# Sample step of the attention moved behind the prompt, its output projection by halves of tokens, and a scaling estimate kept in PSUM

## The chip, the cores and the metric

The kernel runs on one core of a Trainium2 chip. The metric is the device time of one execution in microseconds (us); the number compared is the median over runs. One execution is also recorded by the hardware profiler, and all rows quoted in this document come from such records. Engines are called PE (matrix products; PEld is its loading of weights), DVE (VectorE), ACT (ScalarE), POOL (GpSimd) and SP (SyncE, which issues the DMAs here). SBUF is the on-chip memory of the operands, and PSUM the accumulator memory of eight banks that PE writes and that DVE and ACT read and write.

## The reference

One inference step of a two-layer encoder on 512 prompt tokens and 64 sample tokens (576 in all), width 1024, float32. Layer 0 mixes tokens with a convolution module, layer 1 with stick-breaking attention on shared keys and values; both end in a SwiGLU feed-forward part.

```python
D_MODEL = 1024; SEQ = 512; DEC_SEQ = 64; PAST_LEN = 512
N_HEADS = 16; HEAD_DIM = 64; N_KV_HEADS = 4; GROUP = 4; D_FF = 2816; EPS = 1e-6

def rmsnorm(x, g):
    y = x * lax.rsqrt(jnp.mean(x * x, axis=-1, keepdims=True) + EPS)
    return y * g

def swiglu(xn, w_gu, w_down):
    g, u = jnp.split(xn @ w_gu, 2, axis=-1)
    return (jax.nn.silu(g) * u) @ w_down

def stick_breaking_block(q, k, v, q_pos, k_pos):
    z = jnp.einsum('bgrqd,bgsd->bgrqs', q, k) * (HEAD_DIM ** -0.5)
    mask = k_pos[None, :] < q_pos[:, None]
    log_beta = jax.nn.log_sigmoid(z)
    log_keep = jnp.where(mask, log_beta - z, 0.0)
    after = lax.cumsum(log_keep, axis=4, reverse=True) - log_keep
    att = jnp.where(mask, jnp.exp(log_beta + after), 0.0)
    return jnp.einsum('bgrqs,bgsd->bgrqd', att, v)

# in trunk(), layer 1, once for the prompt and once for the sample tokens:
    h = h + sb_attention(rmsnorm(h, b_norm_g), k_all, v_all, q_pos, k_pos, w_q, w_o)   # o @ w_o at its end
    h = h + swiglu(rmsnorm(h, ffn_norm_g[1]), w_gu, w_down)
    return rmsnorm(h, final_norm_g), ...
```

## The kernel before

Activations lie transposed: a chunk of 128 features on the partitions, the 576 tokens along the row (512 of the prompt, then 64 of the sample). A row is worked on in two halves of 288 tokens, so the second half holds the last 224 prompt tokens and all sample tokens. Each product in float32 precision is made of three in a faster format: every operand is split into a high part (ACT copies it, rounding) and a low part (DVE or POOL subtracts). A weight tile of 512 columns is split in the same way (L518 high part; L528 low part, on DVE). In the feed-forward stages a second copy of the high part is first put into a free PSUM bank (`hp`, L523), so that L528 reads one operand from PSUM; the banks for this are the list `hbanks`, in turn. The feed-forward products use sums of blocks (Strassen's way, seven products in place of eight), which POOL and DVE make (`S`, `ta`, `tb`).

The order of work on each engine is written out ahead: every step is entered as an operation with a cost, the tags that it reads and writes, and a rank; a planner (`Plan`) lays the operations of one stage on the engines by list scheduling, and the engines then run that order. An engine that waits holds up all that stands behind it. An operation that reads two SBUF operands on DVE, or runs on POOL, is entered with `port=True`: the planner doesn't let two such overlap. Stages are planned one after the other: convolution and first feed-forward; keys, values and attention; second output projection and feed-forward.

**Attention.** Ten units run one after another, each in five block steps with the stages z (scores), s (soft-plus), t (running sums), e (weights) and v (times values). A prompt unit `p` does two heads (one group of 128 features, index j = 0 to 7) for 512 tokens; a sample unit `s` does eight heads for the 64 sample tokens, that is, the last 64 columns of four indices j. `S_AT = (4, 7)` puts the sample units behind p3 and ahead of p7, so the order is p0 p1 p2 p3 s0 p4 p5 p6 s1 p7. At its end a unit adds two halves of `av` into the one buffer `oc` (ACT L2276, DVE L2279) and splits `oc` into the operand of the output projection (DVE L2294 `ob`/`oh`, POOL L2297 `ob`/`ol`): one such pair of 512 columns for a prompt unit, four of 64 columns for a sample unit. An output-projection tile `oproj(i, m)` (`pw`) is made of indices 4i to 4i+3 and adds into chunk m of the residual `h` (L759). The eight tiles with i = 0 are spread over the steps of the last two units; those with i = 1 are the mixer of the next stage.

**Entry of the second feed-forward stage.** `ffn(1, ...)` starts from an estimate of the RMS scale: squares of four chunks are summed (`ss0`), a product with ones adds over features (`cs`, banks b6 and b7), ACT turns it into `r0` (Ln L1490, Exp L1494) in an SBUF buffer, and DVE scales each finished chunk with it (`xs`, L1532: chunk, gain column, `r0`). From `xs` come the operands of the gate and up products (L1343 high parts, L1347 low parts). The right scale follows in `rest()`: the sums of all eight chunks go into b6 and b7 (L1505), DVE reads them (`ry`, L1515), multiplies by `r0` twice (L1518), and ACT and DVE make `r`, which is applied after the products. Behind `rest()`, b6 and b7 become the `hp` banks. The first gate and up tile (`pg`) takes the operands in the order of the chunks 0, 4, 1, 5, 2, 6, 3, 7; (1, c) in a tile name is the pair of chunks c and c+4 of stage 1. The next products are `j_A`, `j_B`, `j_C`.

Of the kernel before, what the change touches and what calls it, by code (L numbers as in the profile page):

```python
# [4 lines left out]
F32R = mybir.dt.float32r  # L5
# [65 lines left out]
N_HL = {"s": 4, "e": 3}  # L71
N_T = 6
T_WR = "wr2"
S_AT = (4, 7)
Y_POOL = (2, 4)
LT, LV = 1, 2
Q_AT = 2
# [144 lines left out]
def build(tc, xT, vec, st, stp, bdp, wt, ck, cv, w_in, w_out, gu, down, wk, wv, wq, wo, yT, csp, css, kp, ks, vp, vs):  # L222
# [147 lines left out]
    def pe(n):  # L370
        return n * 0.000442 + 0.004
# [118 lines left out]
    def split_unit(u, tag):  # L490
        kind, i, a, n = units[u]
        th, tl = tag.replace("w", "wh"), tag.replace("w", "wl")
        unit_at[u] = tag
        if kind == "sum":
            sums_of(i, a)
            st = X[("St", i, a)]
            le = LO_S

            def get():
                return X[("S", i, a)][:, :n]  # L500
        else:
# [12 lines left out]

        def hi():
            if not bank:
                place()
            nc.scalar.activation(X[("w", u)][0][:, :n], get(), AF.Copy)  # L518

        def hi_bank():  # L520
            place()
            t = tile(("hp", u), bank, (P, 512), F32R, pool=pp)
            nc.scalar.activation(t[:, :n], get(), AF.Copy)  # L523

        def lo():
            a, b = X[("hp", u) if bank else ("w", u)], X[("w", u)][1]
            a = a if bank else a[0]
            eng(le).tensor_tensor(b[:, :n], get(), a.bitcast(F32)[:, :n], op=ALU.subtract)  # L528
# [35 lines left out]
    def by_part(tag):  # L564
        return [(tag, 0), (tag, 1)]
# [56 lines left out]
    class Norm:  # L622
# [27 lines left out]
        def rstd(self, pair, hf=None, urgent=False, bank=None):  # L650

            key = ("cs", self.name, hf)
            halves = (0, 1) if hf is None else (hf,)
            tag = tuple(pair[q] for q in halves)

            def f():
                X[key] = {q: tile(key + (q,), pair[q], (P, 512), pool=pp) for q in halves}
# [809 lines left out]
    def ffn(l, mixer, g_next, nrm_next, x_busy, k_busy):  # L1467
# [8 lines left out]
        spots["k"] = [t for t in KT if t not in k_busy]  # L1476
        nrm = Norm(f"f{l}")
        cs = ("cs", "f", l)
        r0t = single()
        xt, xops = {}, []  # L1480

        def scale():

            newps(cs, ("b6", "b7"))
            sums_op(cs, ("b6", "b7"), [(lambda: nrm.ss(0), "ss0")])

            def f():
                r0 = spot_tile(("r0", l), r0t)
                for p, (a, n) in zip(full(X[cs]), HALVES):
                    nc.scalar.activation(r0[:, a : a + n], p, AF.Ln, bias=eps, scale=2.0 / D)  # L1490

            def g():
                r0 = X[("r0", l)]
                nc.scalar.activation(r0, r0, AF.Exp, scale=-0.5)  # L1494

            op("ACT", act(T) + 0.19, f, reads=["b6", "b7", "tbl"], writes=by_part(r0t))
            op("ACT", act(T), g, reads=["tbl"], writes=by_part(r0t))

        def rest():

            for i in (0, 1) if l else (1,):

                def f(i=i):
                    for o, (a, n) in zip(full(X[cs]), HALVES):
                        nc.tensor.matmul(o, ones, nrm.ss(i)[:, a : a + n], start=i == 0, stop=True, skip_group_check=True)  # L1505

                op("PE", 8 * pe(HA), f, reads=[f"ss{i}"], writes=["b6", "b7"], bias=99.0)

            def y():
                return X[("ry", l)][:, :T]  # L1510

            def f():
                t = tile(("ry", l), "sq1", (P, 5 * P), pool=base)
                for p, (a, n) in zip(full(X[cs]), HALVES):
                    nc.vector.tensor_scalar(t[:, a : a + n], p, 1.0 / D, EPS, op0=ALU.mult, op1=ALU.add)  # L1515

            def g():
                nc.vector.tensor_tensor(y(), y(), X[("r0", l)], op=ALU.mult)  # L1518

            op("DVE", dve(T) + 0.07, f, reads=["b6", "b7"], writes=["sq1"])  # L1520
            op("DVE", dve(T), g, reads=by_part(r0t), writes=["sq1"], port=True)
            op("DVE", dve(T), g, reads=by_part(r0t), writes=["sq1"], port=True)
            op("ACT", act(T), lambda: nc.scalar.activation(r, y(), AF.Ln), reads=["sq1", "tbl"], writes=both("r"))
            op("ACT", act(T), lambda: nc.scalar.activation(r, r, AF.Exp, scale=-0.5), reads=["tbl"], writes=both("r"))
            newton_step(r, y, T, "sq1", both("r"))
            give(r0t)

        def scaled(m):
            xt[m] = single()

            def f():
                nc.vector.scalar_tensor_tensor(spot_tile(("xs", l, m), xt[m]), h[m], col(V_FG + l * NC + m), X[("r0", l)], op0=ALU.mult, op1=ALU.mult)  # L1532

            op("DVE", dve(T, True), f, reads=H(m) + by_part(r0t), writes=by_part(xt[m]), port=True)

        def x_operands(c):
            res = []
# [21 lines left out]
            for c in (0, 1) if i == 3 and not l else (i // 2,) if i % 2 and (l or i > 3) else ():  # L1559
                x_operands(c)  # L1560
        rest()
        hbanks.extend(("b6", "b7"))
        table("silu_and_others")
        spots["x"] += x_busy
        spots["k"] += k_busy
# [160 lines left out]
    def tail(l, ops_, nrm, finished):  # L1726
# [15 lines left out]
        wi = {q: take() for q in (m, m2)}  # L1742
        for q in (m, m2):
            newps(("pd", q), tag[q])
        op("ACT", 0.0, lambda: nrm.ss(1), writes=both("ss1"))
        op("ACT", 0.0, lambda: tile(("sqc",), "sq1", (P, 5 * P), pool=base), writes=["sq1"])
        for hf, (a, n_) in enumerate(HALVES):
            sl = slice(a, a + n_)
            for q in (m, m2):
# [15 lines left out]
            nrm.rstd(("b6", "b7"), hf, True, ("b5", "b2")[hf])  # L1765
            for q in range(NC // 2):
                yk, yt = ("yo", q, hf), single("xf")

# [570 lines left out]

    todo = []  # L2340

    def oproj(i, m, tag):
        wi = take()
        k = ("pw", i, m)
        newps(k, tag)

        def deps(xk):
            j = xk[1]
            own = by_part(f"k{j - 4}") if 3 < j < 6 else by_part(f"xh{j}") + by_part(f"xl{j}") if j > 5 else []
            return [("ok", j, 0), ("ok", j, SEQ)] + oplace(j) + own  # L2350

        mm_ops(k, tag, wi, [("o", j) for j in range(4 * i, 4 * i + 4)], xdeps=deps)
        add_h(m, k, tag)

    pairs = [("p", t, 4 * t + c) for t in range(2) for c in range(4)]
# [39 lines left out]
    pp = psum_pool("pp3")  # L2395


    ffn(1, lambda i, m: oproj(1, m, (("b0", "b1"), ("b2", "b3"), ("b4", "b5"))[i % 3]), None, Norm("fin"), XT[12:], KT)
    psum.pop().close()
    ctx.close()  # L2400

# [92 lines left out]
```

## Time and profile before

| | |
|---|---|
| median of 3 runs | 1219.28 us (1218.8 to 1220.41) |
| profiled execution, its own time | 1219.93 us |
| its span, first to last instruction | 1218.2 us |
| mean granted PE clock | 0.995 |
| busy: PE, DVE, ACT, POOL | 1190.0, 1016.9, 998.1, 808.6 us |

In the rows of a timeline the columns are start, duration, engine, line, operation, output and inputs, sizes, how many instructions were merged into the row, and in brackets how long the engine sat idle ahead of it and what ended that. In the rows of windows each engine has its busy time and the number of its instructions. In the rows of groups the number behind the bar is the busy time in us, then the mean of one in ns. In the rows of waits the numbers are the total in us, how often, and the longest.

### The profile page before, as it was taken

How to read it: one execution, taken by the hardware profiler on the slowest of the kernel's cores; microseconds unless marked ns; L12 is line 12 of the kernel's file. 1: busy time of each engine (PE TensorE's matmuls, PEld its weight loads, DVE VectorE, ACT ScalarE, POOL GpSimd, SP SyncE). 2: the span in 40 equal slices, each digit the busy share in tenths (PEclk: the TensorE clock that was granted, in tenths of full speed). 3: DMA queues.
4: the chain of work that ended last, by engine and by line, in shares of the span. 5: the costliest groups of instructions: out<-in, count | busy, mean ns of one | idle time of the engine just before them, and what ended most of it. 6: DMA issues, size and time to landing. Idle time of an engine off the chain costs nothing.

```text
span 1218.2 us, 23815 instructions
## 1 busy us (share of the span) xinstructions
PE 1190.0 (98%) x8670; PEld 1161.4 (95%) x8670; DVE 1016.9 (83%) x1643; ACT 998.1 (82%) x1887; POOL 808.6 (66%) x644
## 2 busy tenths in 40 slices
PE   9999989999999999999999999998999999999996
PEld 8999989999999999999999888998999999999996
DVE  6999987979996765998679999979799966668995
ACT  7988474799888887988659999955998889889983
POOL 1999823597867876996204554454699677789951
PEclk9999999999999999999999999999999999999998
DMA  7333822123133323323364322132232424224212
GB/s 270 90 94 93 263 67 86 52 92 117 53 122 105 104 70 94 115 70 106 118 160 105 74 62 74 53 104 59 81 121 71 121 71 122 87 70 123 86 70 78
DMA packets 44997, 121.07 MB, mean 99 GB/s; under 512 B 8784, under 2 KB 14224, under 8 KB 44880
## 3 DMA queue, kind: packets, MB, share of 16 engines
q1 hardware_dynamic: 44880, 119.56, 32.4%
q8 instruction: 68, 1.11, 0.4%
q14 instruction: 49, 0.40, 0.1%
HBM read 105.18 MB, written 5.70 MB: 91 GB/s over the span
## 4 chain that ended last, share of the span: by engine, by line
PE 71%; DVE 11%; POOL 3%; issue 2%; ACT 2%; DMA 1%; SPq 0%; DVEq 0%; POOLq 0%; ACTq 0%
PE j_A L1432 29%; PE j_B L1432 15%; PE j_C L1432 7%; PE po L604 4%; PE b L2226 3%; PE pw L604 3%; PE pq L604 3%; DVE wl L528 2%; DVE acc L1065 2%; PE b L2133 1%; PE av L2253 1%; PE pk L604 1%; DMA qd<-qd 1%; PE pd L604 1%; PE pg L604 1%
## 5 line engine op out<-in xcount | busy, mean ns | idle before, releaser
L518 ACT ACTIVATE wh<-wr 128x512 fp32r<-128x512 f32 (+1 forms) x295 | 178.9, 613 | 34.3 <-PE po L604 15.2
L528 DVE TENSOR_TENSOR wl<-S,hp 128x512 fp32r<-128x512 f32 (+1 forms) x258 | 169.4, 662 | 37.7 <-ACT hp L523 35.0
L528 DVE TENSOR_TENSOR wl<-wr,hp 128x512 fp32r<-128x512 f32 (+1 forms) x233 | 154.2, 666 | 43.2 <-ACT hp L523 39.4
L518 ACT ACTIVATE wh<-S 128x512 fp32r<-128x512 f32 (+1 forms) x260 | 155.7, 610 | 8.1 <-PE j_C L1432 2.9
L523 ACT ACTIVATE hp<-S 128x512 fp32r<-128x512 f32 (+1 forms) x258 | 148.6, 580 | 11.0 <-DVE wl L528 6.3
L523 ACT ACTIVATE hp<-wr 128x512 fp32r<-128x512 f32 (+1 forms) x233 | 134.3, 579 | 16.1 <-DVE wl L528 12.4
L448 POOL TENSOR_TENSOR S<-wr,wr 128x512 f32<-128x512 f32 (+1 forms) x65 | 87.7, 1349 | 86.1 <-ACT wh L518 32.1
L1082 POOL TENSOR_TENSOR pacc<-pacc,pr 128x608 f32<-128x608 f32 x69 | 109.0, 1592 | 7.3 <-ACT pr L1079 4.1
L484 POOL TENSOR_TENSOR S<-wr,S 128x512 f32<-128x512 f32 (+1 forms) x65 | 92.1, 1418 | 26.7 <-DVE wl L528 13.4
L448 POOL TENSOR_TENSOR S<-wr 128x512 f32<-128x512 f32 (+1 forms) x65 | 88.4, 1360 | 21.6 <-ACT wh L518 9.0
L448 POOL TENSOR_TENSOR S<-S,wr 128x512 f32<-128x512 f32 (+1 forms) x65 | 91.3, 1406 | 7.3 <-DVE wl L528 6.5
L1609 POOL TENSOR_TENSOR t<-t,r 128x576 f32<-128x576 f32 x44 | 69.0, 1572 | 3.5 <-ACT t L1580 2.3
L1609 POOL TENSOR_TENSOR a<-a,r 128x576 f32<-128x576 f32 x44 | 70.2, 1599 | 1.1 <-DVE a L1586 1.1
L1065 DVE SCALAR_TENSOR_TENSOR acc<-u,vecs,acc 128x608 f32<-128x608 f32 x76 | 64.6, 850 | 1.0
L1079 ACT ACTIVATE pr<-u,vecs 128x608 f32<-128x608 f32 x69 | 54.0, 795 | 8.3 <-POOL pacc L1082 8.0
L1615 DVE TENSOR_TENSOR a<-a,t 128x576 f32<-128x576 f32 x44 | 52.3, 1188 | 8.1 <-ACT t L1613 7.7
L1580 ACT ACTIVATE t<-j_A 128x288 f32<-128x288 f32 x84 | 34.1, 406 | 23.8 <-PE j_A L1432 22.7
L528 DVE TENSOR_TENSOR wl<-wr,wh 128x512 fp32r<-128x512 f32 x62 | 48.8, 797 | 4.1 <-ACT wh L518 4.0
L2226 PE MATMUL b<-s,sums 128*128 128x512 f32 (+1 forms) x196 | 48.4, 357 | 0.0
L1665 DVE TENSOR_TENSOR h<-j_A,h 128x288 f32<-128x288 f32 x92 | 41.2, 450 | 7.0 <-PE j_A L1432 6.6
L1989 POOL COPY qs<-q 128x64 f32<-128x64 f32 x8 | 3.3, 409 | 56.3 <-DVE q L1986 56.3
L1432 PE MATMUL j_A<-('x', 0, 0)_0_b,wh 128*128 128x288 f32 x168 | 35.7, 295 | 0.5 <-ACT wh L518 0.5
(987 smaller groups left out, 4541.0 us busy)
## 6 DMA issues: line engine op xcount, KB each, us to landing
wr<-gu SPq DMA_DIRECT2D x88, 512.0 KB, 3.6
wr<-down SPq DMA_DIRECT2D x32, 512.0 KB, 3.8
wr<-w_in SPq DMA_DIRECT2D x15, 512.0 KB, 3.9
wm<-wt SPq DMA_DIRECT2D x12, 576.0 KB, 6.3
wr<-down SPq DMA_DIRECT2D x16, 384.0 KB, 3.2
qd<-qd SPq DMA_DIRECT2D x21, 256.0 KB, 2.9
wr<-w_out SPq DMA_DIRECT2D x8, 512.0 KB, 3.8
wr<-wq SPq DMA_DIRECT2D x8, 512.0 KB, 3.6
```

Of the source, the lines that this page charges most:

```text
L448: eng(e).tensor_tensor(t[:, :n], x[1](), y[1](), op=ALU.subtract if sub else ALU.add)
L484: eng(e).tensor_tensor(v[:, :n], X[("raw", i0)][:, n : 2 * n], v[:, :n], op=ALU.subtract)
L518: nc.scalar.activation(X[("w", u)][0][:, :n], get(), AF.Copy)
L523: nc.scalar.activation(t[:, :n], get(), AF.Copy)
L528: eng(le).tensor_tensor(b[:, :n], get(), a.bitcast(F32)[:, :n], op=ALU.subtract)
L604: nc.tensor.matmul(o[hf], (hi, hi, lo)[j][:, s], (xh, xl, xh)[j], start=(start and q == 0 and j == 0), stop=(stop and q == n - 1 and j == ...
L1065: nc.vector.scalar_tensor_tensor(dst, src, wt_, dst if i else X[("kneg",)], op0=ALU.mult, op1=ALU.add)
L1079: nc.scalar.activation(tile(("pr", c, i), f"pr{m}", (P, YW)), src, AF.Copy, scale=wt)
L1082: nc.gpsimd.tensor_tensor(X[("pacc", c)], X[("pacc", c)], X[("pr", c, i)], op=ALU.add)
L1432: nc.tensor.matmul(out, a[:, s], b, start=(start and q == 0 and i == 0), stop=(q == len(ops_) - 1 and i == 2), skip_group_check=True,)
L1609: nc.gpsimd.tensor_tensor(X[k], X[k], r, op=ALU.mult)
L2226: nc.tensor.matmul(out(zz()), X[(w,)], get(x), start=False, stop=(i == len(mms) - 1), skip_group_check=True)
```

## The change

The second sample unit goes to the end: with `S_AT = (4, 8)` the order is p0 p1 p2 p3 s0 p4 p5 p6 p7 s1. Each tile of the second output projection is entered as two groups of 12 matmuls, first half of tokens and then second half; the first half depends on the prompt units alone, and only the second also on the sample unit. In stage 1, `r0` is made and kept in the PSUM tile `c6` (two banks, in the place of b6 and b7), Ln and Exp writing in place; the sums of `rest()` go to b2 and b3 instead; ACT in place of DVE reads them into `ry`; `xs` and the two multiplications of `ry` read `r0` from PSUM and are entered without `port`. When the last reader of `r0` is done, `c6` is taken over as the two `hp` banks. The last norm uses the two halves of `c6` where it used b6 and b7.

```diff
-S_AT = (4, 7)
+S_AT = (4, 8)
...
         def hi_bank():
             place()
-            t = tile(("hp", u), bank, (P, 512), F32R, pool=pp)
+            if isinstance(bank, tuple):
+                X[("hp", u)] = t = X[(bank[0], "hp")][:, bank[1], :]
+            else:
+                t = tile(("hp", u), bank, (P, 512), F32R, pool=pp)
             nc.scalar.activation(t[:, :n], get(), AF.Copy)
...
-        r0t = single()
+        r0t = None if l else single()
+        r0d = both("c6") if l else by_part(r0t)
...
-            newps(cs, ("b6", "b7"))
-            sums_op(cs, ("b6", "b7"), [(lambda: nrm.ss(0), "ss0")])
+            tag = "c6" if l else ("b6", "b7")
+            newps(cs, tag)
+            sums_op(cs, tag, [(lambda: nrm.ss(0), "ss0")])
 
             def f():
+                if l:
+                    X[("r0", l)] = r0 = X[cs][:, O0 : O0 + T]
+                    nc.scalar.activation(r0, r0, AF.Ln, bias=eps, scale=2.0 / D)
+                    return
...
         def rest():
 
+            ck, ct = (("cs2", l), ("b2", "b3")) if l else (cs, ("b6", "b7"))
+            if l:
+                newps(ck, ct)
...
-                for p, (a, n) in zip(full(X[cs]), HALVES):
-                    nc.vector.tensor_scalar(t[:, a : a + n], p, 1.0 / D, EPS, op0=ALU.mult, op1=ALU.add)
+                for p, (a, n) in zip(full(X[ck]), HALVES):
+                    if l:
+                        nc.scalar.activation(t[:, a : a + n], p, AF.Identity, bias=eps, scale=1.0 / D)
+                    else:
+                        nc.vector.tensor_scalar(t[:, a : a + n], p, 1.0 / D, EPS, op0=ALU.mult, op1=ALU.add)
...
-            op("DVE", dve(T), g, reads=by_part(r0t), writes=["sq1"], port=True)
-            op("DVE", dve(T), g, reads=by_part(r0t), writes=["sq1"], port=True)
+            for _ in range(2):
+                op("DVE", dve(T), g, reads=r0d, writes=["sq1"], port=not l)
...
-            op("DVE", dve(T, True), f, reads=H(m) + by_part(r0t), writes=by_part(xt[m]), port=True)
+            op("DVE", dve(T, True), f, reads=H(m) + r0d, writes=by_part(xt[m]), port=not l)
...
         rest()
-        hbanks.extend(("b6", "b7"))
+        if l:
+            op("ACT", 0.0, lambda: tile(("c6", "hp"), "c6", (P, 2, 512), F32R, pool=pp), writes=both("c6"))
+        hbanks.extend(by_part("c6") if l else ("b6", "b7"))
...
-    def oproj(i, m, tag):
+    def oproj(i, m, tag, apart=False):
...
-            return [("ok", j, 0), ("ok", j, SEQ)] + oplace(j) + own
-
-        mm_ops(k, tag, wi, [("o", j) for j in range(4 * i, 4 * i + 4)], xdeps=deps)
+            return [("ok", j, 0)] + [("ok", j, SEQ)] * late + oplace(j) + own
+
+        xs = [("o", j) for j in range(4 * i, 4 * i + 4)]
+        if apart:
+            for hf in range(2):
+                mm_ops(k, tag, wi, xs, halves=(hf,), xdeps=lambda xk, hf=hf: deps(xk, bool(hf)), keep=not hf)
+        else:
+            mm_ops(k, tag, wi, xs, xdeps=deps)
         add_h(m, k, tag)
...
-    ffn(1, lambda i, m: oproj(1, m, (("b0", "b1"), ("b2", "b3"), ("b4", "b5"))[i % 3]), None, Norm("fin"), XT[12:], KT)
+    ffn(1, lambda i, m: oproj(1, m, (("b0", "b1"), ("b2", "b3"), ("b4", "b5"))[i % 3], True), None, Norm("fin"), XT[12:], KT)
```

More of the change, by code (lines that the diff above doesn't have):

```diff
@@ L656, in f @@
             def f():
-                X[key] = {q: tile(key + (q,), pair[q], (P, 512), pool=pp) for q in halves}
+                X[key] = {q: X[pair[q][:1]][:, pair[q][1], :] if isinstance(pair[q], tuple) else tile(key + (q,), pair[q], (P, 512), pool=pp) for q in halves}
             op("PE", 0.0, f, writes=list(tag))
@@ L1494, in g @@
                 nc.scalar.activation(r0, r0, AF.Exp, scale=-0.5)
-            op("ACT", act(T) + 0.19, f, reads=["b6", "b7", "tbl"], writes=by_part(r0t))
-            op("ACT", act(T), g, reads=["tbl"], writes=by_part(r0t))
+            op("ACT", act(T) + 0.19 * (not l), f, reads=tags(tag) + ["tbl"], writes=r0d)
+            op("ACT", act(T), g, reads=["tbl"], writes=r0d)
         def rest():
+            ck, ct = (("cs2", l), ("b2", "b3")) if l else (cs, ("b6", "b7"))
+            if l:
+                newps(ck, ct)
             for i in (0, 1) if l else (1,):
                 def f(i=i):
-                    for o, (a, n) in zip(full(X[cs]), HALVES):
+                    for o, (a, n) in zip(full(X[ck]), HALVES):
                         nc.tensor.matmul(o, ones, nrm.ss(i)[:, a : a + n], start=i == 0, stop=True, skip_group_check=True)
-                op("PE", 8 * pe(HA), f, reads=[f"ss{i}"], writes=["b6", "b7"], bias=99.0)
+                op("PE", 8 * pe(HA), f, reads=[f"ss{i}"], writes=list(ct), bias=99.0)
             def y():
@@ L1513, in f @@
                 t = tile(("ry", l), "sq1", (P, 5 * P), pool=base)
-                for p, (a, n) in zip(full(X[cs]), HALVES):
-                    nc.vector.tensor_scalar(t[:, a : a + n], p, 1.0 / D, EPS, op0=ALU.mult, op1=ALU.add)
+                for p, (a, n) in zip(full(X[ck]), HALVES):
[3 more added lines that the diff above has]
+                        nc.vector.tensor_scalar(t[:, a : a + n], p, 1.0 / D, EPS, op0=ALU.mult, op1=ALU.add)
             def g():
                 nc.vector.tensor_tensor(y(), y(), X[("r0", l)], op=ALU.mult)
-            op("DVE", dve(T) + 0.07, f, reads=["b6", "b7"], writes=["sq1"])
-            op("DVE", dve(T), g, reads=by_part(r0t), writes=["sq1"], port=True)
-            op("DVE", dve(T), g, reads=by_part(r0t), writes=["sq1"], port=True)
+            if l:
+                op("ACT", act(T) + 0.19, f, reads=list(ct), writes=["sq1"])
+            else:
+                op("DVE", dve(T) + 0.07, f, reads=list(ct), writes=["sq1"])
+            for _ in range(2):
+                op("DVE", dve(T), g, reads=r0d, writes=["sq1"], port=not l)
             op("ACT", act(T), lambda: nc.scalar.activation(r, y(), AF.Ln), reads=["sq1", "tbl"], writes=both("r"))
@@ L1525, in rest @@
             newton_step(r, y, T, "sq1", both("r"))
-            give(r0t)
+            if not l:
+                give(r0t)
         def scaled(m):
@@ L1561, in ffn @@
         rest()
-        hbanks.extend(("b6", "b7"))
+        if l:
+            op("ACT", 0.0, lambda: tile(("c6", "hp"), "c6", (P, 2, 512), F32R, pool=pp), writes=both("c6"))
+        hbanks.extend(by_part("c6") if l else ("b6", "b7"))
         table("silu_and_others")
@@ L1744, in tail @@
             newps(("pd", q), tag[q])
+        op("PE", 0.0, lambda: tile(("c6",), "c6", (P, 2, 512), pool=pp), writes=both("c6"))
         op("ACT", 0.0, lambda: nrm.ss(1), writes=both("ss1"))
@@ L1764, in tail @@
                     op("DVE", dve(n_), s, reads=["sq1", ("sq1", hf)], writes=[("ss0", hf)], port=True)
-            nrm.rstd(("b6", "b7"), hf, True, ("b5", "b2")[hf])
+            nrm.rstd(by_part("c6"), hf, True, ("b5", "b2")[hf])
             for q in range(NC // 2):
@@ L2345, in oproj, with deps @@
         newps(k, tag)
-        def deps(xk):
+        def deps(xk, late=True):
             j = xk[1]
             own = by_part(f"k{j - 4}") if 3 < j < 6 else by_part(f"xh{j}") + by_part(f"xl{j}") if j > 5 else []
-            return [("ok", j, 0), ("ok", j, SEQ)] + oplace(j) + own
-        mm_ops(k, tag, wi, [("o", j) for j in range(4 * i, 4 * i + 4)], xdeps=deps)
+            return [("ok", j, 0)] + [("ok", j, SEQ)] * late + oplace(j) + own
[3 more added lines that the diff above has]
+                mm_ops(k, tag, wi, xs, halves=(hf,), xdeps=lambda xk, hf=hf: deps(xk, bool(hf)), keep=not hf)
+        else:
+            mm_ops(k, tag, wi, xs, xdeps=deps)
         add_h(m, k, tag)
```

## The prediction

> **What bounds the kernel now.** I read the page's first part, then the windows by stage, then what PE waited for.
>
> ```profile
> PE 1190.0 (98%) x8670; PEld 1161.4 (95%) x8670; DVE 1016.9 (83%) x1643; ACT 998.1 (82%) x1887; POOL 808.6 (66%) x644
> ...
> 640.00:800.00 160.00, 159.14 (x1019) 142.35 (x1018) 153.16 (x241) 146.32 (x276) 82.27 (x71) 1.00 0.29 73
> 800.00:828.00 28.00, 26.81 (x194) 26.01 (x192) 22.17 (x36) 16.12 (x29) 14.22 (x11) 1.00 0.31 95
> 828.00:850.00 22.00, 18.55 (x125) 16.75 (x125) 22.00 (x39) 12.23 (x24) 9.41 (x6) 1.00 0.21 61
> 850.00:1190.00 340.00, 339.37 (x2558) 338.90 (x2559) 276.04 (x451) 303.63 (x609) 268.72 (x202) 1.00 0.29 93
> ```
>
> The columns of a window are PE, PEld, DVE, ACT, POOL, then PE clock, DMA share and GB/s. PE is busy for 98% of the span, and the change neither adds nor removes a matmul, so it can gain only what PE idles where it works: 0.86 us in the attention stretch (160.00 less 159.14), 1.19 us at its end (28.00 less 26.81), 3.45 us where the feed-forward stage starts (22.00 less 18.55), 0.63 us in the rest of that stage. That is 6.1 us at the very best. In the third of these windows DVE is busy for 22.00 of 22.00. The waits of PE in the two short windows:
>
> ```profile
> PE pg L604 <- DVE ('x', 1, 2)_0_b L1347: 1.7, 1, 1.7
> ...
> PE pw L604 <- POOL ol L2297: 1.2, 1, 1.2
> ...
> PE pg L604 <- DVE ('x', 1, 1)_0_b L1347: 1.1, 1, 1.1
> ...
> PE cs_f L1505 <- DVE ss_f L645: 0.5, 1, 0.5
> ```
>
> So each part of the change has a wait of its own to remove: the new order and the halves the 1.2 us on POOL's `ol`, the estimate in PSUM the 1.1 and 1.7 us on DVE's operands.
>
> **The end of the attention.** The chain behind the last step now, and the cover that PE has for it:
>
> ```profile
> 797.95 0.77 PE L2253 MATMUL av<-e,vv 128*128 128x512 f32 x2
> ...
> 800.46 0.69 PE L604 MATMUL pw<-ob,wh 128*128 128x288 f32 x4
> ...
> 801.25 0.70 PE L604 MATMUL pw<-ob,wh 128*128 128x288 f32 x4
> ...
> 805.49 0.54 PE L604 MATMUL pw<-ol,wh 128*128 128x288 f32 x2 [1.19 <-POOL ol L2297]
> ...
> 790.92 0.77 ACT L2276 ACTIVATE oc<-av 64x256 f32<-64x256 f32 x2
> ...
> 800.58 1.20 ACT L2276 ACTIVATE oc<-av 64x512 f32<-64x512 f32 x2 [2.06 <-POOL ol L2297]
> ...
> 791.79 0.85 DVE L2279 TENSOR_TENSOR oc<-av,oc 64x256 f32<-64x256 f32 x2
> ...
> 793.61 0.29 DVE L2294 CAST ob<-oc 128x64 fp32r<-128x64 f32 x2
> ...
> 795.12 1.24 POOL L2297 TENSOR_TENSOR ob<-oc,ob 128x64 fp32r<-128x64 f32 x2
> ...
> 798.12 0.32 POOL L2297 TENSOR_TENSOR ol<-oc,oh 128x64 fp32r<-128x64 f32 x1
> 798.40 1.41 POOL L645 TENSOR_TENSOR ss_f<-ss_f,sqn_f 128x576 f32<-128x576 f32 x1
> 799.78 0.77 POOL L2297 TENSOR_TENSOR ol<-oc,oh 128x64 fp32r<-128x64 f32 x1
> ...
> 803.80 1.64 POOL L2297 TENSOR_TENSOR ol<-oc,oh 128x512 fp32r<-128x512 f32 x1 [1.86 <-DVE oh L2294]
> ```
>
> p7 ends with `av` at 798.72 (797.95 plus 0.77); its `ol` is ready at 805.44, 6.7 us later, of which ACT loses 2.06 because POOL still reads `oc` for the sample unit that ran just ahead. With s1 last, nothing older sits in `oc`, and the chain is that of the sample unit: ACT 0.77, DVE 0.85, the first cast 0.15 (half of 0.29), four subtractions on POOL 1.24 + 0.32 + 0.77 = 2.33, and for five handovers some 0.1 each (805.44 to 805.49 is the shortest shown): 4.6 us. What covers it: six matmuls take 0.79 us (800.46 to 801.25), so the first halves of three tiles, 36 matmuls, take 4.7 us, and they need nothing of s1. The wait of 1.19 us is then gone. Bounds: if the written order puts only two first halves ahead (3.2 us), 1.4 us of wait stay and 0.2 is lost; if POOL's two sums of squares get between the subtractions as one does now (1.41 each), the chain is 7.4 us, the wait 2.7, and 1.5 us are lost. Above, no more than 1.19 plus a little of the 0.86 is there. I take a gain of **1.0 us**, because both terms nearly balance and the planner sees the same lengths.
>
> The unit itself is moved whole: its z, s, t, e, v steps, its split of q on POOL and its two DMAs that spread q behind it on SP come one unit later, the projection of the last queries stays with p6, and p7 takes its q from there directly, as p5 and p6 do. Such a chain costs PE little now:
>
> ```profile
> PE b L2133 <- DMA qd<-qd: 0.7, 2, 0.4
> ```
>
> I cost it at nothing; the eight tiles of `oproj(0, m)`, spread over the same steps, hide it, and without them one more wait of that sort is 0.4 us. Splitting a tile in halves adds no weight load: PEld has as many instructions as PE already (8670 each).
>
> **The entry of the feed-forward stage.** DVE works without a gap here, and what it spends:
>
> ```profile
> L1532 DVE SCALAR_TENSOR_TENSOR xs<-h,vecs,r 128x576 f32<-128x576 f32 x8 | 8.3, 1050 | 0.0
> L528 DVE TENSOR_TENSOR wl<-wr,wh 128x512 fp32r<-128x512 f32 x7 | 5.9, 854 | 0.0
> ...
> L528 DVE TENSOR_TENSOR wl<-wr,hp 128x512 fp32r<-128x512 f32 x4 | 2.7, 678 | 0.0
> L1518 DVE TENSOR_TENSOR ry<-ry,r 128x576 f32<-128x576 f32 x2 | 2.3, 1145 | 0.0
> ...
> L1515 DVE TENSOR_SCALAR ry<-cs_f 128x288 f32<-128x288 f32 x2 | 0.8, 438 | 0.0
> ...
> L1532 DVE SCALAR_TENSOR_TENSOR xs<-h,vecs,r x8: 800/966/1358, 815.8 to 839.7; 128x576 f32<-128x576 f32 x8
> ```
>
> These are groups of DVE between 810 and 860 us, and the instructions of `xs` (shortest, middle and longest in ns). The same subtraction takes 678 ns with one operand in PSUM and 854 with both in SBUF, and `xs` takes 800 ns alone and up to 1358: two SBUF operands make DVE and POOL hinder each other. With `r0` in PSUM I put `xs` at its 800: 8.3 less 6.4 is 1.9 us. The two reads into `ry` go to ACT, 0.8 us. Together 2.7 us of DVE, all of it ahead of the last of PE's waits, which sum to 2.8. Whether a PSUM operand costs DVE more is shown by
>
> ```profile
> L1780 DVE SCALAR_TENSOR_TENSOR yo<-h,vecs,rb_b x12: 503/505/508, 1206.0 to 1214.1; 128x288 f32<-128x288 f32 x12
> ```
>
> which is the same form with its last operand in PSUM: 505 ns for 288 columns. 288 more cost DVE some 0.31 us (438 ns for 288 in L1515, 0.75 us for 576 in the row of 840.96 below), which makes 815 beside the 800 from SBUF: no more than 0.1 us over all eight. [...]
>
> Against this stands a wait that the change adds. `c6` becomes the `hp` banks only when `ry` has been multiplied twice:
>
> ```profile
> 833.23 0.80 DVE L1515 TENSOR_SCALAR ry<-cs_f 128x288 f32<-128x288 f32 x2
> ...
> 840.96 0.75 DVE L1347 TENSOR_TENSOR ('x', 1, 2)_0_b<-xs,('x', 1, 2)_0_b 128x576 fp32r<-128x576 f32 x1
> ...
> 841.66 0.58 ACT L523 ACTIVATE hp<-S 128x512 fp32r<-128x512 f32 x1
> ...
> 849.85 0.40 PE L1432 MATMUL j_B<-('x', 1, 0)_0_b,wl 128*128 128x288 f32 x1
> ...
> 851.36 0.75 DVE L1518 TENSOR_TENSOR ry<-ry,r 128x576 f32<-128x576 f32 x1
> ...
> 855.36 1.54 DVE L1518 TENSOR_TENSOR ry<-ry,r 128x576 f32<-128x576 f32 x1
> ```
>
> b6 and b7 are free at 834.03 now, the first `hp` copy runs at 841.66, the multiplications at 851.36 and 855.36. They must move to some 842 us or before. Without POOL's hindrance they are 2 x 0.75 = 1.5 us. Ahead of the operand of 840.96 they eat 1.5 of the 2.7 and leave 1.2; behind it they leave 2.7. The `hp` weights feed `j_B` at 849.85 and the operand feeds `pg` at 841.76, so the planner should put the operand first. But PE then comes 3 to 4 us early to weights that ACT and DVE make without a gap:
>
> ```profile
> 845.00:850.00 5.00, 4.89 (x36) 4.51 (x35) 5.00 (x9) 5.00 (x11) 2.34 (x2) 1.00 0.21 52
> ```
>
> That is late next, and gives a part back. Between 1.2 and 2.7 I take **1.9 us**. ACT's two new reads (0.44 each, from the 438 ns of the DVE form) lie in a window where ACT is busy 12.23 of 22.00; were it full, they would cost 0.9. The first of the two sums in `rest()` now waits for L759 to free b2 and b3, ahead of `pg` on PE; the PE wait on `ss_f` (0.5 us) stands at the same place and I leave it as it is. Ln of `r0` as one instruction instead of two is worth 0.2 us on a chain of ACT that I don't count. In the last norm, b6 and b7 or the halves of `c6` are the same two banks to every instruction: nothing.
>
> **The sum.** 1.0 + 1.9 = 2.9 us of PE's idle time. The profiled execution took 1219.93 us, 1.73 more than its span of 1218.2; its span becomes 1215.3, its time 1217.0. It lay 0.65 above the median of the runs, so the median becomes 1219.28 - 2.9 = **1216.4 us**.
>
> **The rivals.** *One half only* (chance 0.33). PE's time saved at one place comes back as a wait at the other, because DVE's chain doesn't follow the earlier PE, or the written order doesn't use the first halves as cover, which is the change not doing what it says. For it: DVE has no gap between 828 and 850, and PE idled 1.19 us at 805 though tiles further on were there. Against: the 2.06 us of ACT behind `oc` vanish by the order of the units alone. With the first term only, 1218.3; with the second only, 1217.4; I give it 1218.0.
>
> *The estimate holds the banks* (chance 0.15), the slower side. If the multiplications stay where they are, the second ends at 856.90; copy 0.58, subtraction 0.68 and handovers of 0.2 bring the first weights at 858.4, 8.5 us after 849.85. Less the 2.9 gained, that is 5.6 us more, 1224.9. It decides from the point where the second multiplication ends after 845.5 (849.85 less 2.9 and 1.5): each us beyond costs one, and beyond 850.8 the kernel is slower by over 0.2%. For it: a DVE that is full. Against: the planner knows the dependence, and `ry` can be ready by 834.
>
> **How the numbers follow.** About 0.2% (2.4 us) is what a measurement of this kernel can tell from no change, so faster means below 1216.8 and slower above 1221.7. Forecast 0.52: its own range, 1.2 to 2.7 plus 1.0 to 1.2 with what is left of 0.86 and 0.63, is 1214.4 to 1217.4; 0.42 of it lies below 1216.8. The first rival gives 0.03 to faster and 0.29 to same with 0.01 slower, the forecast's upper part 0.10 to same, the second rival 0.14 to slower and 0.01 to same. Sum: 0.45 faster, 0.40 same, 0.15 slower. For 8 in 10 the range runs from 1214.4 to 1222.0, into the cheaper part of the second rival.
>
> **What would show it.** Right: PE's wait on `ol` is under 0.3 us, with 36 matmuls of `pw` between the last `av` and the first second-half matmul; `xs` stays near 800 ns in all eight; the waits on `('x', 1, 1)_0_b` and `('x', 1, 2)_0_b` sum to under 1.5 us; the second multiplication of `ry` ends before 845; the 340 us behind 850 keep an idle time near 0.6. Wrong: a new wait on the sample unit's POOL subtractions, PE waiting for `wh` or `wl` for more than 2 us after the first `pg`, or any change of more than 0.5 us ahead of 640 us, where no instruction is touched.

## The result, and the profile after

The changed kernel takes **1230.42 us** (median of 5 runs, 1227.6 to 1231.47), the kernel before, on the same chip, 1218.8 us: a ratio of 1.0095, with an interval of 1.0085 to 1.0106. It is 11.6 us slower, where 2.9 us faster was forecast, and lies outside the range. The profiled execution took 1231.47 us with a span of 1229.8.

The page's first part and the windows of the changed kernel, in the stretches that the prediction used:

```profile
PE 1194.2 (97%) x8670; PEld 1160.3 (94%) x8670; DVE 1010.5 (82%) x1641; ACT 1004.4 (82%) x1888; POOL 800.1 (65%) x644
...
640.00:800.00 160.00, 158.77 (x1014) 141.20 (x1012) 150.46 (x240) 145.39 (x275) 80.55 (x68) 1.00 0.31 75
800.00:828.00 28.00, 27.84 (x200) 27.04 (x201) 24.23 (x47) 17.16 (x30) 12.46 (x14) 1.00 0.33 103
828.00:850.00 22.00, 20.51 (x150) 19.84 (x149) 20.23 (x35) 15.48 (x32) 11.96 (x7) 1.00 0.25 73
850.00:1190.00 340.00, 329.86 (x2445) 324.62 (x2443) 263.12 (x425) 294.65 (x579) 257.24 (x197) 1.00 0.29 91
```

PE's idle time in these four stretches was 0.86, 1.19, 3.45 and 0.63 us; it is now 1.23, 0.16, 1.49 and 10.14. So the two places at which the change aims gained 1.03 and 1.96 us, and the stage behind them lost 9.51 in this window alone. Busy time doesn't tell all of it. The window holds 2445 matmuls in place of 2558, and each counts for a little more busy time (329.86 us by 2445 is 0.135, 339.37 by 2558 is 0.133). At 0.133 us each the 113 that are missing come to some 15 us, an estimate. Within that stage the loss lies in two groups of windows, with little lost between them (0.18 us of idle time from 950 to 1090):

```profile
890.00:910.00 20.00, 19.41 (x147) 19.20 (x146) 17.65 (x24) 16.43 (x33) 18.33 (x13) 1.00 0.19 54
910.00:930.00 20.00, 17.52 (x130) 17.06 (x129) 18.19 (x28) 17.93 (x36) 17.32 (x12) 1.00 0.29 90
...
990.00:1010.00 20.00, 20.00 (x153) 20.00 (x152) 13.10 (x21) 17.93 (x35) 16.48 (x13) 1.00 0.30 102
...
1090.00:1110.00 20.00, 18.41 (x133) 17.52 (x132) 13.46 (x18) 16.02 (x32) 20.00 (x17) 1.00 0.29 83
...
1150.00:1170.00 20.00, 18.58 (x138) 18.14 (x138) 18.86 (x32) 16.41 (x32) 16.77 (x15) 1.00 0.35 106
```

The kernel before has 20.00 of PE in each of these windows but the last (19.46). What PE waits for between 870 and 1190 us in the changed kernel:

```profile
PE j_A L1435 <- DVE a L1607: 4.5, 4, 2.0
PE j_A L1435 <- DVE h L1686: 2.3, 3, 0.9
PE j_B L1435 <- DVE ('a', 1, 2)_3_b L1350: 0.9, 1, 0.9
PE j_A L1435 <- ACT wh L518: 0.7, 2, 0.4
```

These are ordinary partners, late: DVE reads the products out of PSUM late (`a`, `h`), and operands and weights come late. DVE and ACT are what fell behind, though DVE was busy for less time than before (1010.5 against 1016.9 us) and ACT for only 6.3 us more (1004.4 against 998.1). What they wait for is in the view of the tile `c_hp`, the banked copies of the second gate-up stage (840 to 1210 us), here the wait of DVE for the copies and of ACT for DVE's subtraction:

```profile
  ACT c_hp L526: 67.4, 110
  DVE wl L531: 36.1, 83
```

and the same two waits in the kernel before, where the tiles are called `hp`:

```profile
  ACT hp L523: 36.2, 53
  DVE wl L528: 10.0, 20
```

The two engines wait for each other for 103.5 us instead of 46.2, and each of them is left short where it has most to do (DVE 18.19 and ACT 17.93 of 20.00 in the window at 910, with PE idle for 2.48).

**The theory from this.** Before, each banked copy is a tile of one bank, in two banks by turns. Afterwards both banks are halves of one tile, `c6`, and the waits that are put into the program take the tile as a whole: ACT's copy into one half waits until DVE has subtracted from the other, and a subtraction waits for a copy into the other half. Counted from the records, 103 of the 226 copies ran at the same time as a subtraction before, for 33.5 us together; after, none does. In the program's semaphores, 162 of the 226 copies wait for work on the other half (115 for DVE's subtraction, 47 for ACT's own copy), and 47 of the subtractions wait for a copy into the other half; in the kernel before, no copy and no subtraction waits for the other bank. **Rivals:** the estimate in PSUM itself costs (its banks, or its reads); the new order or the halves of tokens bring work to a place where it hinders; or the earlier start of the stage does.

### The profile page after: what moved, and what is told of

Same layout as the page of the kernel before. It is cut to its first block, busy times and chain, and to the rows that moved or that the text cites. A ratio compares the mean times of both kernels' runs of the same rounds, so it can differ in the third digit from the quotient of the medians.

```text
span 1229.8 us, 23801 instructions
## 1 busy us (share of the span) xinstructions
PE 1194.2 (97%) x8670; PEld 1160.3 (94%) x8670; DVE 1010.5 (82%) x1641; ACT 1004.4 (82%) x1888; POOL 800.1 (65%) x644
## 5 line engine op out<-in xcount | busy, mean ns | idle before, releaser
L518 ACT ACTIVATE wh<-wr 128x512 fp32r<-128x512 f32 (+1 forms) x295 | 178.5, 612 | 30.3 <-PE po L607 15.2
L531 DVE TENSOR_TENSOR wl<-S,c_hp 128x512 fp32r<-128x512 f32 (+1 forms) x127 | 83.8, 666 | 30.7 <-ACT c_hp L526 28.4
L531 DVE TENSOR_TENSOR wl<-wr,hp 128x512 fp32r<-128x512 f32 (+1 forms) x134 | 88.9, 667 | 20.9 <-ACT hp L526 19.8
L531 DVE TENSOR_TENSOR wl<-S,hp 128x512 fp32r<-128x512 f32 (+1 forms) x131 | 86.1, 664 | 22.4 <-ACT hp L526 21.6
L531 DVE TENSOR_TENSOR wl<-wr,c_hp 128x512 fp32r<-128x512 f32 (+1 forms) x99 | 65.6, 668 | 39.1 <-ACT c_hp L526 38.9
L526 ACT ACTIVATE c_hp<-S 128x512 fp32r<-128x512 f32 (+1 forms) x127 | 74.2, 584 | 21.0 <-DVE wl L531 18.6
L526 ACT ACTIVATE hp<-wr 128x512 fp32r<-128x512 f32 (+1 forms) x134 | 77.3, 580 | 12.3 <-DVE wl L531 9.4
L526 ACT ACTIVATE hp<-S 128x512 fp32r<-128x512 f32 (+1 forms) x131 | 75.5, 581 | 6.5 <-DVE wl L531 3.4
L526 ACT ACTIVATE c_hp<-wr 128x512 fp32r<-128x512 f32 (+1 forms) x99 | 57.8, 584 | 17.9 <-DVE wl L531 17.5
L1636 DVE TENSOR_TENSOR a<-a,t 128x576 f32<-128x576 f32 x44 | 51.5, 1171 | 12.8 <-ACT t L1634 12.4
```

Of the source, the lines that this page charges most:

```text
L1636: op("DVE", dve(T), lambda: nc.vector.tensor_tensor(X[ku], X[ku], X[kg], op=ALU.mult), reads=by_part(tg), writes=by_part(tu), port=True)
```

## The experiments

**Own tiles, and the shared tile alone.** The first experiment keeps the changed kernel and the order of instructions on every engine, and gives each banked copy a tile of one bank, out of a pool (`pph`) that takes over the place of the estimate's pool (`ppc`). The sums of the last norm, at the end of the kernel, get tiles of their own with it. The second is its mirror image: the kernel before, its order on every engine, with the second stage's copies in the halves of one tile.

```diff
# e1_apart, against the changed kernel
+    def swap():
+        own["ps"].close()
+        own["ps"] = ExitStack()
+        own["hp"] = own["ps"].enter_context(tc.tile_pool(name="pph", bufs=1, space=bass.MemoryType.PSUM, reuse_waits="tile"))
+
-    op("ACT", 0.0, lambda: tile(("c6", "hp"), "c6", (P, 2, 512), F32R, pool=pp), writes=both("c6"))
+    op("ACT", 0.0, swap, writes=both("c6"))
...
-    X[("hp", u)] = t = X[(bank[0], "hp")][:, bank[1], :]
+    t = tile(("hp", u), f"b{6 + bank[1]}", (P, 512), F32R, pool=own["hp"])
# e2_shared, against the kernel before
-    t = tile(("hp", u), bank, (P, 512), F32R, pool=pp)
+    if "hp" not in own:
+        swap()
+        own["hp"] = tile(("c6", "hp"), "c6", (P, 2, 512), F32R, pool=own["b6"])
+    X[("hp", u)] = t = own["hp"][:, int(bank == "b7"), :]
```

> The changed kernel, order of every engine untouched, but each banked copy (hp) is a tile of one bank again; c6 is given back as a whole when its last reader is done, and two separate banks take its place. Theory (one tile): the copies of ACT wait for DVE's subtraction of the OTHER half because both halves are one tile; that alone costs the 16.7 us that the changed kernel loses after its first job. Then the lead of 5.2 us at the first job stays: 1213.6, at most 1216. ACT's wait for wl falls from 36 us to under 20. Rival (order): the loss comes of the new order and of the late release of c6; the time stays at 1228 to 1231.

Measured: 1213.01 us (1212.31 to 1214.41), ratio to before 0.9959 (0.9947 to 0.9972). The same change that cost 11.6 us gains some 5 once the copies have tiles of their own. ACT's wait for the subtractions of this stage falls from 36.1 to 12.4 us.

> The kernel before, order of every engine untouched, but from the second feed-forward stage on the banked copies are the two halves of one tile. Theory (one tile): 12 to 17 us slower than before, 1231 to 1236, ACT waiting some 36 us for wl where it waited 19. Rival (order): 1218.8 as before.

Measured: 1238.68 us (1237.92 to 1244.42), ratio 1.0179 (1.016 to 1.0197). The sign is the theory's, but the time lies above what was expected, so it holds something else. What PE waits for in this run around the last projections:

```profile
PE pw L619 <- DVE oc L2303: 4.7, 1, 4.7
```

No such wait stands in the kernel before. The added pool took banks 6 and 7, so the pool of the stage's other tiles slid down to banks 0 to 5, and its first projection tile came to lie where the attention's sums `av` had been: PE had to wait until `oc` was made from them. That is a side effect of the experiment, so at least 4.7 of the 20.6 us are not the shared tile's, and at most 15.9 are. The wait may cost more than its own length: from 800 to 806 us the granted clock is 0.72 in this run, where it is 1.00 in every run without this wait.

**Each half of the change alone.** The third experiment has the new order and the halves of tokens only (`S_AT = (4, 8)` and the new `oproj`, no estimate in PSUM). The fourth has the estimate in PSUM only, with copies in tiles of their own.

```diff
# e3_order, against the kernel before
-S_AT = (4, 7)
+S_AT = (4, 8)
...
+            for hf in range(2):
+                mm_ops(k, tag, wi, xs, halves=(hf,), xdeps=lambda xk, hf=hf: deps(xk, bool(hf)), keep=not hf)
# e4_psum, against the kernel before
+        r0t = None if l else single()
+        r0d = both("c6") if l else by_part(r0t)
...
+            op("ACT", 0.0, swap, writes=both("c6"))
```

> The kernel before with only the first half of the change: second sample unit last, output projection of heads 4 to 7 by halves; estimate in SBUF, banks b6 and b7 as before. Theory (the two gains are real): PE no longer waits 1.2 us for ol, last pw some 2.3 us earlier, 1216.5 (1215.5 to 1218). Rival (one half only): DVE does not follow, the gain comes back as waits on the gate-up operands, 1218 to 1219.

Measured: 1216.85 us (1216.22 to 1218.42), ratio 0.9991 (0.9982 to 1.0). The halves cost nothing; they gain about 1 us, at the edge of what can be told from none.

> The kernel before with only the second half of the change, with banked copies in tiles of their own: the estimate in PSUM, unit order and projection as before. Theory: xs at 800 ns, the waits on the gate-up operands under 1 us, 2.9 us saved at the first job, 1216 (1215 to 1217.5). Rival (the estimate holds the banks): PE waits for the first banked weights, 1219 or more.

Measured: 1222.17 us (1220.38 to 1226.35), ratio 1.0038 (1.0024 to 1.0051). Taken alone this says that the estimate in PSUM costs 4 us. But the record has the same side effect, with a granted clock of 0.72 from 800 to 806 again:

```profile
PE pw L609 <- DVE oc L2314: 4.7, 1, 4.7
```

So the run decides nothing, and it was made again, together with the two that bear on the shared tile, with the projections left on banks 2 to 7.

**The three again, on the banks that they had.** The two pools are put at opposite ends of PSUM, so `c6` and the copies lie in banks 0 and 1, as in the changed kernel, and the rest in 2 to 7, as before. To that end the pool `ppc` is opened ahead of the stage's other pool.

```diff
# in all three
-        return psum[0].enter_context(tc.tile_pool(name=name, bufs=1, space=bass.MemoryType.PSUM, reuse_waits="tile"))
+        return psum[0].enter_context(tc.tile_pool(name=name, bufs=1, space=bass.MemoryType.PSUM, reuse_waits="tile", side="right" if name == "pp3" else None))
...
# e5_apart2 and e6_psum2; in all three the same for ppc
-tc.tile_pool(name="pph", bufs=1, space=bass.MemoryType.PSUM, reuse_waits="tile")
+tc.tile_pool(name="pph", bufs=1, space=bass.MemoryType.PSUM, reuse_waits="tile", side="left")
```

> The kernel before with identical orders of instructions on every engine, the second gate-up stage's banked copies in the two halves of one tile, nothing else, and the projections on the banks that they had. Theory: the lead at the first job stays at 0 (within 1 us), and then 14 to 18 us are lost, spread as in the changed kernel (about 6 at 870 to 950, about 10 at 1090 to 1205): 1231 to 1236. ACT c_hp waits for wl by 30 to 38 us where the kernel before has 18.7. Rival (the shared tile costs only together with the earlier start or with the estimate's banks): 1222 or less.

Measured: 1234.2 us (1232.82 to 1235.7), ratio 1.0121 (1.0107 to 1.0135): 15.2 us for the shared tile with nothing else changed, inside what the theory gave. The wait on `oc` is gone. The windows of this run, and the waits of the banked copies in it:

```profile
828.00:850.00 22.00, 18.29 (x127) 16.95 (x126) 22.00 (x38) 12.77 (x26) 9.76 (x6) 1.00 0.26 77
850.00:1190.00 340.00, 329.45 (x2444) 324.37 (x2443) 268.55 (x425) 296.51 (x583) 261.69 (x199) 1.00 0.28 92
```

```profile
  ACT c_hp L538: 57.4, 101
  DVE wl L543: 32.6, 79
```

The entry of the stage is as it was before the change (PE idle for 3.71 us there, 3.45 before), and behind it PE idles 10.55 us, as in the changed kernel. No copy overlaps a subtraction. The loss is not spread quite as expected (some 6 us from 870 to 950 and 10 behind 1090): by the matmuls that are missing in the windows it is 3.3 us from 870 to 950, 2.7 from there to 1090 and 9.3 from 1090 to 1205.

> The changed kernel with the same orders of instructions, but each banked copy of the second gate-up stage in a tile of its own of one bank (the same two banks 0 and 1 as in the changed kernel). Theory (the copies and the subtractions of the two banks wait for each other only because both are halves of one tile): ACT's waits for DVE's subtraction fall from 49 us in all to the 19 to 25 us that two tiles had, PE's 20 us slices of 890 to 1190 fill again, 16 to 18 us come back: 1211.5 to 1214. Rival (which two banks the copies lie in is what costs, or the earlier start of the stage is): no more than 4 us come back, 1226 or more. Of the first of these experiments with tiles of their own (1213.01 us, banks 6 and 7) it differs only in the banks; if banks do not matter the two agree within 1.5 us.

Measured: 1213.96 us (1213.3 to 1215.73), ratio 0.9957 (0.9943 to 0.9971). The windows of this run:

```profile
640.00:800.00 160.00, 159.04 (x1017) 141.71 (x1016) 150.12 (x239) 146.48 (x278) 80.40 (x68) 1.00 0.30 73
800.00:828.00 28.00, 27.44 (x197) 26.34 (x196) 23.77 (x46) 16.36 (x29) 14.50 (x15) 1.00 0.33 112
828.00:850.00 22.00, 20.51 (x151) 20.04 (x151) 21.20 (x38) 15.48 (x31) 10.30 (x6) 1.00 0.22 72
850.00:1190.00 340.00, 340.00 (x2565) 339.88 (x2565) 273.99 (x449) 302.75 (x605) 264.54 (x200) 1.00 0.29 91
```

PE doesn't idle at all between 850 and 1190. The same orders, the same two banks and the same early start of the stage are 16.7 us apart from the changed kernel (11.6 above and 5.1 below their own runs of before), by the tiles' declaration. The sums of the last norm changed their tiles too, but the 120 matmuls that this window holds more are nearly all of it, some 15.9 us. The copies' two waits are 39.8 and 12.7 us here, near the 36.2 and 10.0 of the kernel before. Which two banks the copies lie in doesn't matter either: in banks 6 and 7 the ratio was 0.9959. How the waiting looks is seen in a few microseconds of ACT and DVE in the changed kernel:

```profile
851.33 0.60 ACT L526 ACTIVATE c_hp<-S 128x512 fp32r<-128x512 f32 x1
...
853.71 0.60 ACT L526 ACTIVATE c_hp<-S 128x512 fp32r<-128x512 f32 x1 [0.70 <-DVE wl L531]
854.34 0.60 ACT L526 ACTIVATE c_hp<-wr 128x512 fp32r<-128x512 f32 x1
...
851.96 0.69 DVE L531 TENSOR_TENSOR wl<-wr,c_hp 128x512 fp32r<-128x512 f32 x1 [1.20 <-ACT c_hp L526]
852.57 0.45 DVE L1607 TENSOR_TENSOR a<-j_A,a 128x288 f32<-128x288 f32 x1
852.94 0.68 DVE L531 TENSOR_TENSOR wl<-S,c_hp 128x512 fp32r<-128x512 f32 x1
855.05 0.69 DVE L531 TENSOR_TENSOR wl<-S,c_hp 128x512 fp32r<-128x512 f32 x1 [1.43 <-ACT c_hp L526]
```

and the same instructions with tiles of their own:

```profile
851.66 0.60 ACT L528 ACTIVATE hp<-wr 128x512 fp32r<-128x512 f32 x1
852.19 0.60 ACT L528 ACTIVATE hp<-S 128x512 fp32r<-128x512 f32 x1
...
853.77 0.58 ACT L528 ACTIVATE hp<-S 128x512 fp32r<-128x512 f32 x1
854.29 0.58 ACT L528 ACTIVATE hp<-wr 128x512 fp32r<-128x512 f32 x1
...
852.30 0.69 DVE L533 TENSOR_TENSOR wl<-wr,hp 128x512 fp32r<-128x512 f32 x1 [0.50 <-ACT hp L528]
852.91 0.45 DVE L1615 TENSOR_TENSOR a<-j_A,a 128x288 f32<-128x288 f32 x1
853.27 0.68 DVE L533 TENSOR_TENSOR wl<-S,hp 128x512 fp32r<-128x512 f32 x1
854.39 0.69 DVE L533 TENSOR_TENSOR wl<-S,hp 128x512 fp32r<-128x512 f32 x1 [0.43 <-ACT hp L528]
```

In the shared tile the copy at 853.71 starts when the second subtraction of the pair before it has ended (852.94 plus 0.68 is 853.62), though its own bank was free from 852.65; and the first subtraction, at 851.96, starts when the second copy has ended (851.33 plus 0.60). With tiles of their own the first subtraction (852.30) runs beside the second copy (852.19 to 852.79). From one pair of copies to the next (854.34 less 851.33, 854.29 less 852.19) it is 3.0 us against 2.1. In the run with own tiles 99 copies run beside a subtraction, in the very banks in which none does in the changed kernel, and they are no slower for it: the copies have medians of 589 and 592 ns (602 in the changed kernel), the subtractions of 676 and 677 (681 and 686). So the memory asked for no such waits.

> The kernel before with the estimate r0 in PSUM alone (edit B: Ln and Exp there, two ry reads on ACT, pools so that the last projections keep the banks that they had), copies in tiles of their own, no halves of tokens and S_AT as before. Theory (B is worth the 1.9 us that the prediction gave it, and the 1222.17 us of the earlier run with this edit came from a projection tile that had slid onto the banks of the attention sums and cost 4.7 us there): 1215.5 to 1217.5, with the first job matmul 1.5 to 2.5 us earlier than before. Rival (B does not pay without the halves): 1218.5 or more, with no new PE wait for oc at the last projection.

Measured: 1216.76 us (1215.01 to 1218.8), ratio 0.998 (0.9971 to 0.9989). Its windows:

```profile
800.00:828.00 28.00, 26.81 (x193) 25.93 (x192) 22.59 (x43) 16.04 (x29) 12.54 (x10) 1.00 0.32 111
828.00:850.00 22.00, 19.68 (x143) 19.00 (x142) 21.32 (x37) 15.30 (x32) 10.17 (x6) 1.00 0.23 72
850.00:1190.00 340.00, 340.00 (x2565) 339.90 (x2565) 272.61 (x449) 303.00 (x604) 265.66 (x201) 1.00 0.28 91
```

The estimate in PSUM gains about 2.3 us without the halves, and leaves the end of the attention as it was (26.81 in both). Its first version has the same instructions in the same order and differs from it only in where the pools lie, so the banks made the difference to 1222.17 us. The wait on `oc` is not all of that: the recorded execution, the slowest of the six, also has a wait of PE of 3.3 us between 1090 and 1110, whose cause is open. Together:

| against before | copies in tiles of their own | copies in halves of one tile |
|---|---|---|
| no other change | 1 | 1.0121 |
| order and halves of tokens | 0.9991 | |
| estimate in PSUM | 0.998 | |
| both | 0.9957 | 1.0095 (the change) |

The kernel of the last row with tiles of their own is faster than both the kernel before and the changed one.

## Why the prediction was wrong

**The end of the attention: 1.0 us.** The mechanism was right, the cover was smaller than put. The wait of 1.19 us on `ol` is gone, and what is left there in the changed kernel is

```profile
PE pw L607 <- DVE ob L2316: 0.4, 1, 0.4
PE av L2275 <- POOL e L2107: 0.4, 1, 0.4
```

Between the last `av` and the first product that needs s1 there are 18 matmuls, not 36: the written order has one first half of a tile and half of another there, and then already the second half of the first tile. POOL's two sums of squares did come ahead of the subtractions (3.38 us for the two, from 796.67), but the chain was still as long as put (4.4 us, from the end of `av` at 797.37 to that of the last `ob` at 801.79, against 4.6). PE takes s1's operands one after another and so waited 0.4 us for the first of them only. The stretch of the attention idles 1.23 us instead of 0.86, but 0.26 of these are the beginning of this wait, which starts at 799.74; what is left for the unit "moved whole" is about 0.1, near the nothing that was put. The two stretches together gained 0.66 us of idle time where 1.0 was put, and the runs with this part alone gave 0.9991.

**The entry of the feed-forward stage: 1.9 us.** Right in its terms, but for ACT's two reads, which were put at 0.44 us each and took 0.50.

```profile
L1551 DVE SCALAR_TENSOR_TENSOR xs<-h,vecs,cs_f x8: 799/802/805, 812.5 to 833.7; 128x576 f32<-128x576 f32 x8
...
L1528 ACT ACTIVATE ry<-cs,eps x2: 502/504/506, 831.2 to 831.7; 128x288 f32<-128x288 f32 x2
L1533 DVE TENSOR_TENSOR ry<-ry,cs_f x2: 744/744/744, 835.1 to 839.5; 128x576 f32<-128x576 f32 x2
...
PE pg L607 <- DVE ('x', 1, 2)_0_b L1350: 1.5, 1, 1.5
```

`xs` stays at its 800 ns in all eight, the reads into `ry` run on ACT, the second multiplication ends at 840.3 (it starts at 839.54), ahead of 845, and the wait on `('x', 1, 1)_0_b` has gone while that on `('x', 1, 2)_0_b` is 1.5 us. PE idles 1.96 us less. With `r0` in PSUM the median of the eight is 802 ns, where the shortest from SBUF took 800, so even the 15 ns more for each that the prediction worked out (815 beside 800) don't show.

**What the two gave together.** The first `j_A` matmul, which is the same instruction of PE in all runs, shows how early PE comes out of the entry. Part of its lead stands at 640 already, ahead of anything that the edits touch; it is counted here in matmuls at 0.133 us each, so the last column is an estimate.

| against before | first `j_A` matmul earlier | matmuls ahead at 640 | lead without these |
|---|---|---|---|
| changed kernel | 5.2 us | 14 | 3.3 |
| order and halves alone | 4.7 | 22 | 1.8 |
| estimate alone | 3.6 | 13 | 1.9 |
| shared tile alone | 1.8 | 14 | 0.0 |
| both, own tiles | 3.4 | 2 | 3.1 |

So up to the first `j_A` the sum of 2.9 us held; PE's idle time alone shows 2.62 us (0.66 and 1.96).

**"But PE then comes 3 to 4 us early to weights that ACT and DVE make without a gap".** PE did come 3.3 us early. The part back was not asked for where the copies have tiles of their own: there the 340 us behind 850 idle 0.00, and even the 0.63 of before is won.

**The step that failed** is a term that the sum doesn't have. The prediction followed `c6` to the point at which the `hp` banks become free, and of the last norm it said that "b6 and b7 or the halves of `c6` are the same two banks to every instruction: nothing". It took the same for granted of the 226 copies, for which it has no term. To the memory they are the same two banks; to the waits they are one tile. That term measured 15.2 us on the kernel before and 16.7 on the changed one, against the 2.9 that was forecast as gain. It could have been bounded from the trace of before, in the rows of the copies and subtractions of this stage:

```profile
L523 ACT ACTIVATE hp<-S x127: 468/591/624, 841.7 to 1187.3; 128x512 fp32r<-128x512 f32 x111, 128x384 fp32r<-128x384 f32 x16
L528 DVE TENSOR_TENSOR wl<-S,hp x127: 532/676/690, 845.7 to 1187.9; 128x512 fp32r<-128x512 f32 x111, 128x384 fp32r<-128x384 f32 x16
L523 ACT ACTIVATE hp<-wr x99: 469/592/612, 846.0 to 1193.5; 128x512 fp32r<-128x512 f32 x87, 128x384 fp32r<-128x384 f32 x12
L528 DVE TENSOR_TENSOR wl<-wr,hp x99: 539/676/692, 847.0 to 1194.1; 128x512 fp32r<-128x512 f32 x87, 128x384 fp32r<-128x384 f32 x12
```

226 copies of 0.59 us and as many subtractions of 0.68 are some 287 us that must not overlap within about 350, on two engines that have other work between; before, 33.5 us of them did overlap. So the cost, as an estimate, lies between 0 and some 33.5 us; PE paid about half of that. With the row of this one term the range would have reached far to the slower side.

**The rivals.** "The estimate holds the banks" had the right side and the right tile, but not the mechanism: it decides only if the second multiplication ends after 845.5, and it ended at 840.3. "One half only" came in part with the order alone, whose windows are

```profile
828.00:850.00 22.00, 18.96 (x132) 17.49 (x131) 22.00 (x36) 14.09 (x29) 11.73 (x7) 1.00 0.24 73
850.00:1190.00 340.00, 338.72 (x2550) 338.01 (x2551) 275.16 (x449) 301.58 (x604) 264.55 (x200) 1.00 0.29 91
```

DVE is still full at the entry, and PE idles 1.28 us behind it where it idled 0.63 before: that is given back. With the estimate in PSUM and own tiles nothing is, so the two gain more together (about 5 us) than alone (1.2 and 2.3). Whether that is all of the difference is open; the intervals are 2 to 3 us wide. Of the signs named, the 0.6 us of idle time behind 850 was the one that spoke of the loss. The sign for the stretch ahead of 640 was a poor one: PE's busy time there, with no instruction of that stretch touched, is

```profile
0.00:640.00 640.00, 627.87 (x4654) 620.26 (x4655) 527.97 (x846) 512.04 (x938) 429.25 (x352) 1.00 0.37 111
```

in the record of before and 628.73 to 630.86 in those of all the other runs, that with the identical order and the shared tile alone (629.94) among them; so records differ there by up to 3 us.

## What to carry to other kernels

When buffers are merged into one tile, ask what else is put into the merged tile later, and count how often its parts are in use at the same time: what ran side by side in two tiles ran in turn in one here (103 of 226 copies beside a subtraction before, none after), and the trace of before shows the overlap that is at stake. In this kernel two engines that hand a pair of buffers back and forth need two tiles, even where these lie in the same banks as the halves of one (1213.96 us against 1230.42). Where PE is nearly always busy, count its matmuls in a window too: its busy time showed only 9.51 of some 15 us. A pool added for an experiment can move everything else to other banks (here PE then waited 4.7 us for `oc`), so look for new waits far from the edit before the difference is read as the edit's.

## What the runs showed of the hardware that was not expected

ACT's scaled read of 288 columns from PSUM with a bias (`ry`) takes 502 to 506 ns, where its plain copies of 288 columns from PSUM take 0.39 to 0.42 us in the same stage; the prediction had put it at 0.44. ACT's banked copies have a median of 602 ns where they never run beside a subtraction, and 591 where 103 of them do; the subtractions, 681 and 686 against 676. So in two banks the two engines don't slow each other in any way that these rows show.
